# Attention in units of 32 queries of all eight heads that share keys and values

## The chip, the cores and the metric

The kernel runs on one core of a Trainium2 chip. The metric is the device time of one execution in microseconds (us), 794.44 as the median of three runs of the kernel before. A core has five engines with a queue each, which run side by side and wait for each other by semaphores: TensorE (PE; its weight loads are shown as PEld), VectorE (DVE), ScalarE (ACT), GpSimd (POOL) and SyncE (SP, which issues DMAs).

## What is computed

One layer: a norm, attention over a sliding window of 128 keys, a gated output projection, an embedding stage with a gate, and a last norm. 512 positions of width 2048, 32 query heads of 64, four heads of keys and values, so that eight query heads share each (`SWA_GROUP`). What the change touches is the attention and the projection of its queries:

```
q, k, v, gate = jnp.split(h @ w_in, [...], axis=-1)
q = q.reshape(bsz, nb, BLOCK, SWA_KV_HEADS, SWA_GROUP, SWA_HEAD_DIM)
...
scores = jnp.einsum('bnqhgd,bnjhd->bnhgqj', q, kb).astype(jnp.float32) * (SWA_HEAD_DIM ** -0.5) + bias
scores = jnp.where(mask, scores, jnp.finfo(jnp.float32).min)
m = jnp.maximum(scores.max(axis=-1, keepdims=True), sink)
e = jnp.exp(scores - m)
probs = e / (e.sum(axis=-1, keepdims=True) + jnp.exp(sink - m))
out = jnp.einsum('bnhgqj,bnjhd->bnqhgd', probs.astype(vb.dtype), vb).reshape(bsz, seq, SWA_WIDTH)
return (out * jax.nn.silu(gate)) @ w_out
```

A query sees itself and the 127 keys before it.

## The kernel before

Nearly every product is taken three times, with operands split in a high and a low part (`mm3`, lines 123 to 128: high by high, high by low, low by high). ScalarE makes the high part (a cast), VectorE the low part (a subtraction).

*Start.* A loop over 16 slices of the input projects the first two pairs of query heads, all keys (`kt`) and all values, up to 71 us. A pair of heads is one "c" of 16. `evac_q` (line 315) takes a projected pair from PSUM in three parts: `scaled` on VectorE, then the high parts on ScalarE and the low ones on VectorE, into the tile `Q[d]` of two pairs (four heads).

*Projections and attention together.* `projections()` walks over the other 14 query pairs and 16 gates; `kinds` gives their order. One step is one slice of the 2048 rows, three matmuls of 512 columns; a projection has 16 steps. Its weights come in pieces of 8 steps: a DMA of 512 KB into one of three buffers (`wraw`), a cast (`whi`, L109) and a subtraction (`wlo`, L110). What must be done once a projection ends are `chores` of three parts: of a query pair those of `evac_q`, of a gate a product on VectorE (L626), a tanh on ScalarE (L627) and a product on VectorE (L620).

Attention is cut into 64 units of 64 queries of four heads: eight groups `d` of four heads, with eight units `g` each. A loop of 67 rounds (`for i in range(blocks + 3)`) writes the order of the engines out by hand. After 16 steps ahead, a round holds

- `turn(i - 2)`: two transposes of a unit's probabilities (`pt`), ScalarE's high and VectorE's low part (`r`), a masked copy of it for queries whose window crosses a block's end (`own`, GpSimd's `affine_select`, then a copy of half of it on ScalarE, L567);
- `weigh(i - 3)`: values' products, stationary V, moving `r`, 256 columns: high, low, and one with `own` where there is one (48 units of 64); after every second unit the two halves are added into `U` (L594, L596);
- `scores(i)`: two products, stationary 32 queries of four heads, moving up to 160 keys with high and low parts side by side (320 columns), then bias, minimum, exponential, reciprocal and, a round later, the product with the reciprocal (`pr`, L532);
- seven projection steps, and between them a weight piece, chores, the later parts of the above, and DMAs that copy and sum weights in DRAM for the output stages (`sum_weights`).

PE, SP, DVE, ACT and POOL all follow the written order here. `gate_value` (L610) multiplies a gate with `U` as soon as both are there. Then come two stages of matmuls with the output and gate weights (`unit`, `Pieces`), where a scheduler orders ScalarE and VectorE.

*Buffers.* `whole` has four quarters of 8 KB a partition: after the first norm they hold `misc` (bias vector, first queries), `values`, `diffs` (differences of neighbouring value blocks, for `own`) and later the four gates. Tile `t` (scores) has three buffers, `pr` three, `r` and `own` two, `U` three.

Of the kernel before, what the change touches and what calls it, by code (L numbers as in the profile page):

```python
# [11 lines left out]
F32 = mybir.dt.float32  # L12
F32R = mybir.dt.float32r
AF = mybir.ActivationFunctionType
ALU = mybir.AluOpType
# [12 lines left out]

TWOS = PAIRS // 2
HB = P // 2  # L30
UNITS = S // HB
QB = P // 4
# [23 lines left out]
def trunk_kernel(ctx: ExitStack, tc: tile.TileContext, a: dict):  # L56
# [74 lines left out]
    sinkb = const.tile([P, TWOS], F32, name="sinkb")  # L131
# [49 lines left out]
    q_at = {int(0.5 + 3.516 * (c // 2)) - 3 + c % 2: c for c in range(2, PAIRS)}  # L181
    kinds, g = [], 0
    for m in range(2 * PAIRS - 2):
        if m in q_at:
            kinds.append(("q", q_at[m]))
        else:
            kinds.append(("g", g))
            g += 1
# [10 lines left out]
    for k in range(KC):  # L199
# [106 lines left out]
        if k == 10:  # L306
            for h in range(4):
                nc.sync.dma_start(sinkb[QB * h : QB * h + QB], a["sinks"][h].partition_broadcast(QB))
            nc.sync.dma_start(pn, a["ple_norm"])
# [5 lines left out]
    def evac_q(c, ps, to=None):  # L315


        to = ps if to is None else to
        d, u = divmod(c, 2)
        if u == 0:  # L320
            Q[d] = kvq.tile([P, S // QB, 4, QB], F32R, tag="q", name=f"q{d}", bufs=2)
        halves = slice(0, 64), slice(64, 128)

        def scaled():
            nc.vector.scalar_tensor_tensor(out=to, in0=ps, scalar=HD ** -0.5, in1=rb, op0=ALU.mult, op1=ALU.mult)

        def split(low):
            for e in range(2):
                src = to[halves[e]].rearrange("p (s q) -> p s q", q=QB)
                hi, lo = Q[d][halves[e], :, 2 * u + e], Q[d][halves[1 - e], :, 2 * u + e]  # L330
                if low:
                    nc.vector.tensor_sub(lo, src, hi.bitcast(F32))
                else:
                    nc.scalar.copy(hi, src)

        return scaled, partial_of(split, False), partial_of(split, True)
# [10 lines left out]
    misc = quarter("misc")  # L347
    first_q = [evac_q(c, q_ps[c], misc[:, 3 * c]) for c in range(2)]
# [35 lines left out]
    full = quarter("values").rearrange("p k (t c) -> p (k t) c", t=2)  # L384
# [10 lines left out]
    relb, tvec = misc[:HEADS, 1, :BUCKETS], misc[:HEADS, 2, :TOEP]  # L395
# [23 lines left out]
    U, T, PT, O, gates, biases = {}, {}, {}, {}, {}, {}  # L419
# [3 lines left out]
    diffs = {}  # L423

    def make_diff(n):
        if n == 1:
            diffs["all"] = quarter("diffs").rearrange("p k t -> p (k t)")
# [25 lines left out]
    def load_bias(d):  # L453
        biases[d] = apool.tile([P, KEYS], F32, tag="bias", name=f"bias{d}", bufs=2)
        for h in range(4):
            src = bass.AP(
                tensor=tdram.tensor, offset=tdram.offset + (4 * d + h) * TOEP + P - QB, ap=[[1, QB], [1, KEYS]]
            )
            nc.sync.dma_start(biases[d][QB * h : QB * h + QB], src)

    def scores(i):
# [6 lines left out]
        if g == 4 and d + 1 < TWOS:  # L468
            load_bias(d + 1)
        of_keys = K[d // 2].rearrange("p j l k -> p (j l k)")  # L470

        s_ps = spsum.tile([P, 2, S], F32, tag="w", name=f"s{i}")
        number = [min(2 * g + u + 1, 5) * QB for u in range(2)]
        for u in range(2):
            first, n = max(2 * g + u - 4, 0), number[u]
            st = Q[d][:, 2 * g + u].rearrange("p h q -> p (h q)")
            nc.tensor.matmul(s_ps[:, u, : 2 * n], st, of_keys[:, first * 2 * QB : (first * QB + n) * 2], start=True, stop=True)  # L477
        W = KEYS + 2
        t = apool.tile([P, 2, W], F32, tag="t", name=f"t{i}", bufs=3)
# [9 lines left out]
        late = QB if g >= 2 else 0  # L489
# [9 lines left out]
        if g < 2:  # L499
# [14 lines left out]
        if g >= 2:  # L514
# [11 lines left out]
        T[i] = apool.tile([P, 2, P], F32, tag="pr", name=f"pr{i}", bufs=3)  # L526
        for u in range(2):
            out, src = T[i][:, u], pr[u]
            if late and (g + u) % 2:
                out = out.rearrange("p (h k) -> p h k", h=2)[:, ::-1]  # L530
                src = src.rearrange("p (h k) -> p h k", h=2)
            nc.scalar.mul(out, src, sm[:, 4 + u : 5 + u])  # L532

    def turn(i):
# [8 lines left out]
        r = apool.tile([P, 2, 256], F32R, tag="r", name=f"r{i}", bufs=2)  # L543
        rh, rl = (r[:, l].rearrange("p (h u q) -> p u h q", h=4, u=2) for l in range(2))
        src = pt.rearrange("p (u h q) -> p u h q", u=2, h=4)
# [3 lines left out]
        own = None  # L549
        if g >= 2:  # L550
            own = apool.tile([P, 2, 256], F32R, tag="own", name=f"own{i}", bufs=2)
            rows = slice(0, P) if g % 2 else slice(0, HB)
            flat = lambda v: v[rows].rearrange("p l (u q) -> p (l u) q", q=HB)


            sign = -1 if g % 2 else 1
            nc.gpsimd.affine_select(  # L557
                out=flat(own), in_=flat(r).bitcast(F32), pattern=[[0, 8], [sign, HB]], compare_op=ALU.is_ge, fill=0.0,
                base=-HB - 1 if g % 2 else 0, channel_multiplier=-sign,
            )  # L560
        PT[i] = (r, own)
        yield
        if own is not None:
            here, there = slice(HB, P), slice(0, HB)
            if g % 2 == 0:
                here, there = there, here
            nc.scalar.copy(own[there, 0], own[here, 1].bitcast(F32))  # L567

    def weigh(i):

        d, g = divmod(i, UNITS)
        n, b = divmod(g, 2)
        kv = d // 2
        r, own = PT.pop(i)
        if g == 0:
            U[d] = apool.tile([P, 2, S], F32, tag="u", name=f"u{d}", bufs=3)
        if b == 0:
            O[d] = bank(f"o{i}", "o").rearrange("p (b u e q) -> p b u e q", b=2, u=2, e=2)
        ops = O[d]
        out = ops[:, b].rearrange("p u e q -> p (u e q)")  # L580
# [8 lines left out]
        if b:  # L589
            dst = U[d][:, :, n * P : (n + 1) * P].rearrange("p u (b q) -> p b u q", b=2)  # L590
            lower, upper = slice(0, 64), slice(64, 128)
            tmp = [apool.tile([P, 2, 2, HB], F32, tag=f"tmp{e}", name=f"tmp{e}_{i}", bufs=1) for e in range(2)]
            for e, (o, x) in enumerate(((lower, upper), (upper, lower))):
                nc.scalar.copy(tmp[e][o], ops[x, :, :, e, :])  # L594
            for e, o in enumerate((lower, upper)):
                nc.vector.tensor_add(dst[o], ops[o, :, :, e, :], tmp[e][o])  # L596
        if g == UNITS - 1:
            for c in (2 * d, 2 * d + 1):
# [8 lines left out]
    def gate_value(c):  # L607
# [3 lines left out]
            out=src, in0=src, scalar=0.5, in1=U[c // 2][:, c % 2], op0=ALU.mult, op1=ALU.mult  # L611
# [260 lines left out]

    nc.scalar.mul(sinkb, sinkb, -1.0)  # L873
# [3 lines left out]
    for n in range(KC):  # L877
# [3 lines left out]
    blocks = TWOS * UNITS  # L881
# [11 lines left out]
    left = KC * (len(kinds) - 1)  # L893

    def some(of, n=1):
        for _ in range(min(n, len(of))):
            of.pop(0)()

    softmax = iter(())
    for i in range(blocks + 3):  # L900
# [3 lines left out]
        value = weigh(i - 3) if 3 <= i else iter(())  # L904
        next(turned, None)
        next(value, None)
# [504 lines left out]
def laid_out(i):  # L1411
# [28 lines left out]
        "sinks": f(np.asarray(i["swa_sinks"])[0].reshape(TWOS, 4).T),  # L1440
# [19 lines left out]
```

## Time and profile before

| | |
|---|---|
| median of 3 runs (793.89 to 794.51) | 794.44 us |
| the profiled execution | 794.82 us |
| its span, first to last instruction | 793.1 us |
| granted TensorE clock | 0.997 |
| DMA moved | 185.23 MB, 234 GB/s on average |

A page of the profile gives each engine's busy time, the chain of work that ended last, and groups of equal instructions with count, busy time and mean. A row of a timeline reads: start in us from the span's start, duration, engine, line, operation, out<-in, shape, count. Rows of matmuls overlap in time, since one starts before the one ahead has drained. "[x <-y]" is idle time of the engine before the row and what ended it. The rows themselves stand in the prediction.

### The profile page before, as it was taken

The numbers are of one execution on the slowest core, as the hardware profiler recorded it, in microseconds if no ns is written. First come the engines' busy times: TensorE is split into PE (matmuls) and PEld (weight loads), VectorE is DVE, ScalarE is ACT, GpSimd is POOL, SyncE is SP. The second block draws the span as 40 slices with busy tenths as digits, with TensorE's granted clock in tenths as the row PEclk, the third lists the DMA queues.
The fourth block names the chain that finished last, engine by engine and source line by source line (L and its number), as shares of the span: only waits on it lengthen the run. The fifth ranks groups of instructions, "written<-read, shape, count | busy, mean of one in ns | idle before, by whom it ended". The sixth has DMA issues, their size and how long they took to land.

```text
span 793.1 us, 11181 instructions
## 1 busy us (share of the span) xinstructions
PE 783.2 (99%) x3746; PEld 656.0 (83%) x3746; DVE 585.7 (74%) x1155; ACT 506.7 (64%) x1067; POOL 148.5 (19%) x248
## 2 busy tenths in 40 slices
PE   9999999999999999999999999999999999999995
PEld 8888888888888888888888888888888888888885
DVE  4547587867867587767777899778866757988896
ACT  6743576666767586766666654466699656656765
POOL 0200423242413324132324200000000120210000
PEclk9999999999999999999999999999999999999998
DMA  9977999897989989898987498667864996787533
GB/s 349 275 215 264 207 275 303 223 267 215 277 227 269 223 249 258 230 247 235 244 227 182 140 365 337 197 212 232 275 237 142 346 203 202 157 225 220 176 107 106
DMA packets 45066, 185.23 MB, mean 234 GB/s; under 512 B 6656, under 2 KB 7680, under 8 KB 39888
## 3 DMA queue, kind: packets, MB, share of 16 engines
q1 hardware_dynamic: 36928, 143.30, 53.0%
q0 software_dynamic: 8080, 41.22, 27.1%
q8 instruction: 29, 0.48, 0.2%
q14 instruction: 29, 0.24, 0.1%
HBM read 177.63 MB, written 62.97 MB: 303 GB/s over the span
## 4 chain that ended last, share of the span: by engine, by line
PE 99%; DVE 0%; ACT 0%; ACTq 0%; issue 0%; DVEq 0%
PE gps L126 7%; PE gps L127 7%; PE gps L128 7%; PE qps L126 7%; PE qps L127 7%; PE qps L128 7%; PE o L127 6%; PE g L128 6%; PE g L127 5%; PE o L126 5%; PE o L128 5%; PE g L126 5%; PE s L477 2%; PE o L583 2%; PE vps L290 2%; PE pt L541 2%
## 5 line engine op out<-in xcount | busy, mean ns | idle before, releaser
L728 DVE TENSOR_TENSOR blo<-braw,bhi 128x1024 fp32r<-128x1024 f32 x102 | 124.4, 1222 | 40.9 <-ACT bhi L727 40.6
L727 ACT CAST bhi<-braw 128x1024 fp32r<-128x1024 f32 x102 | 107.3, 1052 | 72.2 <-PE o L128 24.8
L126 PE MATMUL gps<-xh,whi 128*128 128x512 f32 x256 | 100.0, 390 | 0.0
L127 PE MATMUL gps<-xl,whi 128*128 128x512 f32 x256 | 99.9, 390 | 0.0
L128 PE MATMUL gps<-xh,wlo 128*128 128x512 f32 x256 | 99.8, 390 | 0.0
L126 PE MATMUL qps<-xh,whi 128*128 128x512 f32 x224 | 87.8, 392 | 0.0
L127 PE MATMUL qps<-xl,whi 128*128 128x512 f32 x224 | 87.4, 390 | 0.0
L128 PE MATMUL qps<-xh,wlo 128*128 128x512 f32 x224 | 87.3, 390 | 0.0
L110 DVE TENSOR_TENSOR wlo<-wraw,whi 128x1024 fp32r<-128x1024 f32 x60 | 73.7, 1229 | 6.1 <-ACT whi L109 5.9
L547 DVE TENSOR_TENSOR r<-pt,r 128x256 fp32r<-128x256 f32 x64 | 27.2, 424 | 66.5 <-ACT r L546 65.6
L546 ACT CAST r<-pt 128x256 fp32r<-128x256 f32 x64 | 23.9, 373 | 80.9 <-PE pt L541 80.8
L126 PE MATMUL g<-bhi,fhg 128*128 128x512 f32 x192 | 75.1, 391 | 0.0
L126 PE MATMUL o<-bhi,fho 128*128 128x512 f32 x192 | 74.8, 390 | 0.0
L128 PE MATMUL g<-bhi,flg 128*128 128x512 f32 x192 | 74.8, 389 | 0.0
L127 PE MATMUL o<-blo,fho 128*128 128x512 f32 x192 | 74.8, 389 | 0.0
L128 PE MATMUL o<-bhi,flo 128*128 128x512 f32 x192 | 74.7, 389 | 0.0
L127 PE MATMUL g<-blo,fhg 128*128 128x512 f32 x192 | 74.7, 389 | 0.0
L557 POOL TENSOR_SCALAR_AFFINE_SELECT own<-r 64x512 fp32r<-64x512 f32 (+1 forms) x48 | 32.5, 677 | 224.6 <-DVE r L547 208.7
L109 ACT CAST whi<-wraw 128x1024 fp32r<-128x1024 f32 x60 | 62.2, 1039 | 5.4 <-issue 4.0
L492 POOL COPY t<-sinkb 128x2 f32<-128x2 f32 x64 | 53.2, 839 | 57.7 <-ACT sinkb L873 32.4
L707 POOL DMA_DIRECT2D grown<-in_ple_gate x16 | 13.8, 861 | 231.0 <-DVE blo L728 226.7
L128 PEld LDWEIGHTS gps<-xh,wlo 128*128 128x128 f32 x256 | 48.1, 188 | 10.3
(228 smaller groups left out, 1800.3 us busy)
## 6 DMA issues: line engine op xcount, KB each, us to landing
wraw<-in_w_gate_in SPq DMA_DIRECT2D x32, 512.0 KB, 6.5
w_out<-in_w_out POOLq DMA_DIRECT2D x32, 512.0 KB, 8.0
braw<-w_out SPq DMA_DIRECT2D x32, 512.0 KB, 4.4
wraw<-in_w_q SPq DMA_DIRECT2D x28, 512.0 KB, 5.3
braw<-in_ple_gate SPq DMA_DIRECT2D x24, 512.0 KB, 4.1
braw<-in_w_out SPq DMA_DIRECT2D x22, 512.0 KB, 4.2
xw<-in_first SPq DMA_DIRECT2D x14, 640.5 KB, 6.4
w_out<-in_w_out SPq DMA_DIRECT2D x16, 512.0 KB, 10.1
```

Source lines behind the costliest of these rows:

```text
L109: nc.scalar.copy(hi, raw)
L110: nc.vector.tensor_sub(lo, raw, hi.bitcast(F32))
L126: nc.tensor.matmul(ps, sh, mh, start=first, stop=False, skip_group_check=more)
L127: nc.tensor.matmul(ps, sh, ml, start=False, stop=False, skip_group_check=more)
L128: nc.tensor.matmul(ps, sl, mh, start=False, stop=last, skip_group_check=more)
L290: nc.tensor.matmul(v_ps[t], h[:, c], part_of(high_at, 256, 512), start=f, stop=e, skip_group_check=True)
L492: nc.gpsimd.tensor_copy(two(0, W + W - 1 if late else W, 1), sinkb[:, d : d + 1].unsqueeze(1).to_broadcast([P, 2, 1]))
L546: nc.scalar.copy(rh, src)
L547: nc.vector.tensor_sub(rl, src, rh.bitcast(F32))
L557: nc.gpsimd.affine_select(out=flat(own), in_=flat(r).bitcast(F32), pattern=[[0, 8], [sign, HB]], compare_op=ALU.is_ge, fill=0.0, base=-HB ...
L727: nc.scalar.copy(hi, raw)
L728: nc.vector.tensor_sub(lo, raw, hi.bitcast(F32))
```

## The change

Units become 32 queries of all eight heads that share keys and values: four groups `kv` with 16 units each, again 64 units. A score product has 16 queries of eight heads as stationary operand, and sees up to 144 keys (288 columns). Two units together make 64 queries of eight heads, and their values' products take 512 columns at once, every second round. `evac_q` now gathers four pairs of heads; for groups 0 and 2 the queries lie in two quarters of `whole`, which doubles the number of instructions for the parts. The order of the projections changes: all queries of the first group come first, 40 steps instead of 16 stand ahead of the loop, and a round holds six steps up to round 21 and seven from then on. In a round the values' products stand ahead of the transposes.

```diff
+GROUP = HEADS // KVH
+QB = P // GROUP
+TQ = 2 * QB
+UNITS = S // TQ
...
+    order = "qqqqqgqggqgqqqggqgqqqg" + "g" * 8
...
-        d, u = divmod(c, 2)
+        kv, u = divmod(c, 4)
         if u == 0:
-            Q[d] = kvq.tile([P, S // QB, 4, QB], F32R, tag="q", name=f"q{d}", bufs=2)
+            if kv % 2:
+                tiles = [kvq.tile([P, 4 * S * 2], F32R, tag="q", name=f"q{kv}")]
+            else:
+                tiles = [quarter(f"q{kv}_{n}").rearrange("p k t -> p (k t)").bitcast(F32R) for n in range(2)]
+            Q[kv] = [v.rearrange("p (s h q) -> p s h q", h=GROUP, q=QB) for v in tiles]
...
             for e in range(2):
+                for part, of in enumerate(Q[kv]):
...
-        number = [min(2 * g + u + 1, 5) * QB for u in range(2)]
+        number = [min(2 * g + u + 1, GROUP + 1) * QB for u in range(2)]
...
-        t = apool.tile([P, 2, W], F32, tag="t", name=f"t{i}", bufs=3)
+        t = apool.tile([P, 2, W], F32, tag="t", name=f"t{i}", bufs=2)
...
-            out, src = T[i][:, u], pr[u]
-            if late and (g + u) % 2:
+            out, src, w = T[i][:, u], pr[u], sm[:, 4 + u : 5 + u]
+            ahead = 2 * (g + u) % GROUP * QB if late else 0
+            if ahead == P // 2:
                 out = out.rearrange("p (h k) -> p h k", h=2)[:, ::-1]
...
+            else:
+                nc.scalar.mul(out[:, ahead:], src[:, : P - ahead], w)
+                if ahead:
+                    nc.scalar.mul(out[:, :ahead], src[:, P - ahead :], w)
...
-        r = apool.tile([P, 2, 256], F32R, tag="r", name=f"r{i}", bufs=2)
+        j, part = divmod(i, 2)
+        if part == 0:
+            own = None
+            if g >= P // TQ:
+                own = apool.tile([P, 2, S], F32R, tag="own", name=f"own{j}")
+            PT[j] = apool.tile([P, 2, S], F32R, tag="r", name=f"r{j}"), own
...
-    def weigh(i):
+    def weigh(j):
...
+        out = bank(f"o{j}", "o")
         first = V[0 if n == 0 else n - 1 + b][:, kv]
         for low in range(2):
             nc.tensor.matmul(out, first, r[:, low], start=low == 0, stop=own is None and low == 1)
...
-    for n in range(KC):
+    AHEAD = 5 * KC // 2
+    for n in range(AHEAD):
         next(proj)
         if n % 4 == 3 and W.todo:
             W.todo.pop(0)()
-    blocks = TWOS * UNITS
+        if n > KC and n % 2:
+            some(chores)
+    blocks = KVH * UNITS
...
-        value = weigh(i - 3) if 3 <= i else iter(())
+        value = weigh(i // 2 - 2) if 4 <= i and i % 2 == 0 else iter(())
+        next(value, None)
         next(turned, None)
-        next(value, None)
         next(softmax, None)
```

What this makes of the queues, at three places. First TensorE, before, at the start of a round in the second group of heads (`gps` and `qps` are projections, `s` scores):

```order
L128 MATMUL gps_1608<-xh_492,wlo_1597 128x512
L541 MATMUL pt_1697<-ident,pr_1648 128x128 x2
L583 MATMUL o_1703<-r_1631,V_716 128x256 x2
L585 MATMUL o_1703<-own_1646,DV 128x256
L477 MATMUL s_1707<-k_721,q_1022 128x320 x2
L126 MATMUL gps_1608<-xh_528,whi_1596 128x512
```

and in the changed kernel the starts of rounds 24 and 25, the first with the values of two units, the second with none:

```order
L586 MATMUL o_2376<-r_2262,V_730 128x512 x2
L588 MATMUL o_2376<-own_2261,DV 128x512
L546 MATMUL pt_2380<-ident,pr_2332 128x128 x2
L478 MATMUL s_2396<-k_1362,q_1086 128x288 x2
L126 MATMUL qps_2307<-xh_492,whi_2285 128x512
```

```order
L128 MATMUL qps_2446<-xh_142,wlo_2347 128x512
L546 MATMUL pt_2451<-ident,pr_2402 128x128 x2
L478 MATMUL s_2456<-k_1362,q_1086 128x288 x2
L126 MATMUL qps_2446<-xh_184,whi_2346 128x512
L127 MATMUL qps_2446<-xl_185,whi_2346 128x512
```

Values' products moved from every round to every second, ahead of the transposes, with twice the columns.

Second ScalarE, before, in a round with a weight cast, the high parts of a query pair and the copy of `own`:

```order
L546 CAST r_2196<-pt_2193 128x2x4x32
L532 ACTIVATE pr_2210<-t_2139,sm_2146 128x128
L532 ACTIVATE pr_2210<-t_2139,sm_2146 128x2x64
L109 CAST whi_2223<-wraw_2155 128x1024
L334 CAST q_2034<-qps_2035 64x16x32 x2
L567 CAST own_2208<-own_2208 64x256
```

and in the changed kernel in round 25:

```order
L557 CAST r_2384<-pt_2451 128x2x8x16
L535 ACTIVATE pr_2462<-t_2399,sm_2406 128x128
L535 ACTIVATE pr_2462<-t_2399,sm_2406 128x96
L537 ACTIVATE pr_2462<-t_2399,sm_2406 128x32
L109 CAST whi_2476<-wraw_2414 128x1024
L336 CAST q_0_2136<-qps_2307 64x16x16
L336 CAST q_1_2137<-qps_2307 64x16x16
L336 CAST q_0_2136<-qps_2307 64x16x16
L336 CAST q_1_2137<-qps_2307 64x16x16
L574 CAST own_2383<-own_2383 64x8x32
```

The high parts, still ahead of the copy of `own`, are four casts instead of two.

Third VectorE in the same two rounds. Before, from the end of the round ahead (its reciprocal is L523):

```order
L596 TENSOR_TENSOR u_2071<-o_2072,tmp_17_2169 64x2x2x64
L325 SCALAR_TENSOR_TENSOR qps_2035<-qps_2035,rb 128x512
L523 RECIPROCAL sm_2146<-sm_2146 128x2
L547 TENSOR_TENSOR r_2196<-pt_2193,r_2196 128x2x4x32
L507 TENSOR_TENSOR t_2206<-s_2203,bias_1636 128x2x160
```

and in the changed kernel within round 25:

```order
L516 TENSOR_TENSOR t_2459<-t_2459 128x2x16
L110 TENSOR_TENSOR wlo_2477<-wraw_2414,whi_2476 128x1024
L325 SCALAR_TENSOR_TENSOR qps_2307<-qps_2307,rb 128x512
L334 TENSOR_TENSOR q_0_2136<-qps_2307,q_0_2136 64x16x16
L334 TENSOR_TENSOR q_1_2137<-qps_2307,q_1_2137 64x16x16
```

The scaling of the query pair (L325), on which the high parts wait, stood a round ahead of them and now stands behind the weight split of the same round. In round 41 it is the same with two casts of 64x32x16.

More of the change, by code (lines that the diff above doesn't have):

```diff
@@ L177, in rsqrt_mean @@
         nc.vector.tensor_mul(out, y, t)
[L181 to L188, printed above, removed]
+    order = "qqqqqgqggqgqqqggqgqqqg" + "g" * 8
+    number = {"q": iter(range(2, PAIRS)), "g": iter(range(PAIRS))}
+    kinds = [(kind, next(number[kind])) for kind in order]
+    assert len(kinds) == 2 * PAIRS - 2
     for kind, c in kinds:
@@ L306, in trunk_kernel @@
         if k == 10:
-            for h in range(4):
+            for h in range(GROUP):
                 nc.sync.dma_start(sinkb[QB * h : QB * h + QB], a["sinks"][h].partition_broadcast(QB))
@@ L498, in scores @@
         sm = apool.tile([P, 24], F32, tag="sm", name=f"sm{i}", bufs=4)
-        if g < 2:
+        if not late:
             for u, n in enumerate(number):
@@ L513, in scores @@
             )
-        if g >= 2:
+        if late:
             nc.vector.tensor_tensor(
@@ L564, in turn @@
             here, there = slice(HB, P), slice(0, HB)
-            if g % 2 == 0:
+            if not b:
                 here, there = there, here
-            nc.scalar.copy(own[there, 0], own[here, 1].bitcast(F32))
-    def weigh(i):
[L571 to L580, printed above, removed]
+            nc.scalar.copy(flat(own, there)[:, :GROUP], flat(own, here)[:, GROUP:].bitcast(F32))
+    def weigh(j):
+        kv, m = divmod(j, S // HB)
+        n, b = divmod(m, 2)
+        r, own = PT.pop(j)
+        if m == 0:
+            U[kv] = apool.tile([P, 4, S], F32, tag="u", name=f"u{kv}", bufs=2)
+        out = bank(f"o{j}", "o")
         first = V[0 if n == 0 else n - 1 + b][:, kv]
@@ L588, in weigh @@
         yield
[L589 to L598, printed above, removed]
+        ops = out.rearrange("p (u e q) -> p u e q", u=4, e=2)
+        dst = U[kv][:, :, m * HB : (m + 1) * HB]
+        lower, upper = slice(0, 64), slice(64, 128)
+        tmp = [apool.tile([P, 4, HB], F32, tag=f"tmp{e}", name=f"tmp{e}_{j}") for e in range(2)]
+        for e, (o, x) in enumerate(((lower, upper), (upper, lower))):
+            nc.scalar.copy(tmp[e][o], ops[x, :, e, :])
+        for e, o in enumerate((lower, upper)):
+            nc.vector.tensor_add(dst[o], ops[o, :, e, :], tmp[e][o])
+        if m == S // HB - 1:
+            for c in range(4 * kv, 4 * kv + 4):
                 weighed.add(c)
@@ L871, in projections, with some @@
                 yield
+    def some(of, n=1):
+        for _ in range(min(n, len(of))):
+            of.pop(0)()
     nc.scalar.mul(sinkb, sinkb, -1.0)
@@ L891, in sums_in @@
         return range(SUMS_EARLY + (i - 4) * n // of, SUMS_EARLY + (i - 3) * n // of)
[L893 to L897, printed above, removed]
+    left = KC * len(kinds) - AHEAD
     softmax = iter(())
```

77 lines of the change are left out of this document (36 added, 41 removed).

## The prediction

> **What bounds it now.** First the page and the list of TensorE's waits.
>
> ```profile
> span 793.1 us, 11181 instructions
> PE 783.2 (99%) x3746; PEld 656.0 (83%) x3746; DVE 585.7 (74%) x1155; ACT 506.7 (64%) x1067; POOL 148.5 (19%) x248
> PE 99%; DVE 0%; ACT 0%; ACTq 0%; issue 0%; DVEq 0%
> PE warm_ps L141 <- PEq L1450: 0.8, 1, 0.8
> ```
>
> TensorE is busy for 99% of the span, the chain that ended last is TensorE throughout, and its only listed wait is 0.8 us at the start. So a matmul saved is time saved, unless another engine then makes TensorE wait. Next I read one whole round, from the transposes of one unit to those of the next, in the timeline.
>
> ```profile
> 299.60 0.38 PE L541 MATMUL pt<-ident,pr 128*128 128x128 f32 x2
> 299.73 0.48 PE L583 MATMUL o<-r,V 128*128 128x256 f32 x2
> 300.05 0.28 PE L585 MATMUL o<-own,DV 128*128 128x256 f32 x1
> 300.17 0.46 PE L477 MATMUL s<-k,q 128*128 128x320 f32 x2
> 300.47 0.39 PE L126 MATMUL qps<-xh,whi 128*128 128x512 f32 x1
> ...
> 305.02 0.40 PE L128 MATMUL qps<-xh,wlo 128*128 128x512 f32 x1
> 305.26 0.38 PE L541 MATMUL pt<-ident,pr 128*128 128x128 f32 x2
> ...
> 305.71 0.28 PE L585 MATMUL o<-own,DV 128*128 128x256 f32 x1
> 305.83 0.34 PE L477 MATMUL s<-k,q 128*128 128x64 f32 x2
> ...
> 306.29 0.39 PE L127 MATMUL qps<-xl,whi 128*128 128x512 f32 x1
> ...
> 776.65 0.28 PE L126 MATMUL last<-last,fhg 128*128 128x256 f32 x1
> ...
> 780.60 0.28 PE L126 MATMUL last<-last,fhg 128*128 128x256 f32 x1
> ```
>
> Durations overlap here, so I price a matmul by the distance between starts. The 21 projection matmuls from 300.47 to 305.02 stand 4.55/20 = 0.2275 us apart; the 34 matmuls of 256 columns from 776.65 to 780.60 stand 3.95/33 = 0.1197 us apart. A straight line through both is 0.0119 us plus 0.000421 us a column: 0.1466 for 320 columns (the row shows (300.47 - 300.17)/2 = 0.15) and 0.1332 for 288. Very short products don't follow it: 64 and 128 columns take 306.29 - 305.83 - 0.2275 = 0.23 us together, about 0.115 each.
>
> **The change, part by part.**
>
> *Score products.* 96 products of 320 columns become 96 of 288: 96 x (0.1466 - 0.1332) = 1.29 us saved. The first products of each group of heads are 32 before and 32 after; before, 16 are of up to 128 columns (0.23 a pair) and 16 of 192 or 256; after, they go from 32 to 256. At 0.115 to 0.12 apiece both sums are 3.7 us: nothing.
>
> *Values' products.* 128 + 48 = 176 of 256 columns become 64 + 24 = 88 of 512: 176 x 0.1197 - 88 x 0.2275 = 1.05 us saved. [...]
>
> *Transposes* stay 128. A short matmul followed by a weight load costs extra: behind the transposes this round spends 299.73 to 300.05 on two products that are worth 0.24, 0.08 us too much. After the change the score product stands there. The trace has such rounds:
>
> ```profile
> 92.40 0.38 PE L541 MATMUL pt<-ident,pr 128*128 128x128 f32 x2
> 92.53 0.54 PE L477 MATMUL s<-k,q 128*128 128x320 f32 x2
> ...
> 97.70 0.38 PE L541 MATMUL pt<-ident,pr 128*128 128x128 f32 x2
> ```
>
> There the round takes 5.30 us, 21 x 0.2275 + 4 products on the line (2 x 0.066 + 2 x 0.1466) = 5.20 and 0.10 too much: the same extra, nothing saved. **TensorE's own work falls by 1.29 + 1.05 = 2.34 us**, call it 2.3.
>
> *New rounds.* Rounds without value products (odd ones) now alternate with rounds that carry 512-column ones. Those up to 21 hold six projection steps, later ones seven. By the row above, an odd round of seven steps takes 5.30 - 2 x 0.0134 = 5.27 us, one of six 4.59. The second unit of a pair gets its masked copy ("own") in the odd round, and the third matmul of the next round reads it: at 5.27 + 2 x 0.2275 = 5.73 us after the odd round's transposes (5.05 with six steps). Before, it was due at 305.71 - 299.60 = 6.11. So ScalarE has 0.38 us less. What it does in such a round:
>
> ```profile
> 300.01 0.38 ACT L546 CAST r<-pt 128x256 fp32r<-128x256 f32 x1 [1.76 <-PE pt L541]
> 300.28 0.69 ACT L532 ACTIVATE pr<-t,sm 128x128 f32<-128x128 f32 x2
> 300.88 1.04 ACT L109 CAST whi<-wraw 128x1024 fp32r<-128x1024 f32 x1
> 304.01 0.60 ACT L627 ACTIVATE gps<-gate 128x512 f32<-128x512 f32 x1 [2.09 <-DVE gate L626]
> 304.64 0.40 ACT L567 CAST own<-own 64x256 fp32r<-64x256 f32 x1
> ...
> 302.16 1.22 DVE L110 TENSOR_TENSOR wlo<-wraw,whi 128x1024 fp32r<-128x1024 f32 x1
> 303.29 0.68 DVE L626 TENSOR_TENSOR gate<-gps,rb 128x512 f32<-128x512 f32 x1
> ...
> 133.44 0.69 DVE L325 SCALAR_TENSOR_TENSOR qps<-qps,rb 128x512 f32<-128x512 f32 x1
> 134.17 1.18 ACT L334 CAST q<-qps 64x512 fp32r<-64x512 f32 x2 [1.45 <-DVE qps L325]
> ...
> L594 ACT COPY tmp<-o 64x256 f32<-64x256 f32 x64 | 23.5, 367 | 1.1
> ...
> 77.25 0.20 ACT L873 ACTIVATE sinkb<-sinkb 128x8 f32<-128x8 f32 x1
> ```
>
> The copy L567 stands behind the tanh L627, that waits for VectorE's L626, and that for the weight split L110: it ends at 305.04, 5.44 us after the transposes, 0.67 ahead of its reader. In the order of the changed kernel two odd rounds of seven steps have, behind the weight split, the scaling of a query projection on VectorE and its high parts on ScalarE, and only then the copy:
> - round 41, two casts of 64x512: 5.44 + (1.18 - 0.60) = 6.02, due at 5.73: **0.3 us of waiting**;
> - round 25 (the one shown in the order), four casts of 64x256 because this group's queries lie in two tiles. The nearest row is L594, 0.367 each: 5.44 + (1.47 - 0.60) = 6.31: **0.6 us**.
> In round 57 a tanh stands there as above: 5.44 against 5.73, no wait. In round 7 (six steps) the scaling is a round earlier, but the round before is full (weights, two key casts, two copies): I put the end at 4.9 to 5.1 against 5.05: 0 to 0.1. These waits, about **1.0 us**, are paid in full, since TensorE has nothing else queued. Bounds: zero, if the casts are shorter than L594's, and 1.8, if each costs what half of L334 does (0.59).
>
> *Edits at no cost.* A late unit's probabilities take three ScalarE instructions instead of two in 48 units. The 8-column row L873 took 0.20, so this adds 0.2 to 0.3 us a unit ahead of the weights' cast; VectorE, busy until 302.16 in that round, hides it, and without this cover it would add to the two waits. The first round starts 40 steps into the projections instead of 16:
>
> ```profile
> 71.47 0.39 PE L126 MATMUL gps<-xh,whi 128*128 128x512 f32 x1
> ...
> 82.36 0.33 PE L477 MATMUL s<-k,q 128*128 128x64 f32 x2
> ...
> 457.02 1.28 DVE L610 SCALAR_TENSOR_TENSOR gate<-gate,u 128x512 f32<-128x512 f32 x2
> 458.22 1.22 DVE L728 TENSOR_TENSOR blo<-braw,bhi 128x1024 fp32r<-128x1024 f32 x1
> ...
> 460.73 0.39 PE L127 MATMUL o<-blo,fho 128*128 128x512 f32 x1
> ```
>
> 16 steps took 10.89 us, so the last of the four queries that the first scores need is projected 32 steps in, and 8 steps (5.4 us) are left for its scaling (0.69), a weight pair (1.04 + 1.22) and its high parts (4 x 0.37, with the low ones close behind on VectorE): about 4.4, no wait. At the end four gate products fall behind the last unit instead of two, 1.28 us more on VectorE ahead of a weight split that had 460.73 - 459.44 = 1.29 us to spare; in the changed order one weight split and one form of 0.6 to 1.2 us move away from there, so about zero, at worst 0.5. Pools with fewer buffers (t, pr, r, own) are refilled one or two rounds after their last reader; the value products were moved ahead of the transposes, so the single r is free when ScalarE refills it.
>
> **Sum.** The profiled execution took 794.82 us (span 793.1). 794.82 - 2.3 + 1.0 = 793.5; it lay 0.4 above the median 794.44, so I forecast **793.2**.
>
> **Rivals.**
> - *No new wait*: the casts are quick enough, or an order of 0.1 us in each queue helps. Only the 2.3 count: 792.1. For it: no wait behind the copy is listed now. Against: 0.3 and 0.6 are missing by rows of this trace.
> - *More waits than two*: rounds of six steps are short for ScalarE, and each backlog of some 0.3 us in rounds 7, 15 and the end's 0.5 adds up to another 1.0: 794.2.
> - *Width doesn't pay*: 512 columns cost two of 256, so the change doesn't do what it says. Then only the scores gain: 1.3 saved, 1.0 waited: 794.1. Against it are the starts 0.1197 and 0.2275 apart. [...]
> - *Slower: the DMAs can't keep up with shorter rounds.* Copies and sums of weights are issued by round, and rounds 4 to 21 shrink from 305.26 - 299.60 = 5.66 us to 4.59 without and 4.59 + 3 x 0.2275 = 5.27 with value products, 4.93 on average, 13% less.
>
> ```profile
> 160.00:180.00 20.00, 20.00 (x101) 16.82 (x100) 13.27 (x42) 13.92 (x41) 9.93 (x17) 1.00 0.96 270
> ...
> 200.00:220.00 20.00, 20.00 (x100) 16.78 (x99) 16.02 (x44) 15.59 (x41) 8.35 (x14) 1.00 0.97 295
> ...
> L109 ACT CAST whi<-wraw 128x1024 fp32r<-128x1024 f32 x54 | 56.1, 1038 | 0.0
> ...
> DMA to landing us min/median/max: 4.5/9.2/14.4
> ```
>
> The DMA share is 0.96 in the first row. If the 0.97 of the second is all that can be carried, 0.96 x 5.66/4.93 = 1.10 stretches 18 rounds (89 us) by 13%, 12 us; with half of it, as the projections' weights are not issued by round, 794.44 - 2.3 + 1.0 + 6 = 799. It decides once a weight lands later than its cast is due. A weight lasts 8 steps, 8/7 of 5.66 = 6.5 us; three buffers less a split of 2.3 leave 17 us, and the longest landing is 14.4. Against: the cast L109 never waited (0.0 over 54).
>
> **Numbers.** A measurement of this kernel can tell about 0.2% (1.6 us) from no change; the line lies at 792.85. Forecast 0.45 (793.2, of it 0.07 below the line), no wait 0.27, more waits 0.12, width 0.06, slower 0.10. Faster 0.07 + 0.27 = 0.34, slower 0.10, same 0.56. The range runs from 791.8 (no wait, 0.3 of scatter) to 795.4 (waits at their bound of 1.8, the end's 0.5 and 1.0 of further ones).
>
> **What would show it.** Starts of 512-column value products 0.227 apart, scores 0.133; "o <- ACT own" in TensorE's waits, some 0.6 us near 228 us and 0.3 near 317 us, nothing elsewhere in the loop; L109 still without idle time. The prediction is wrong if those waits are absent or other ones stand in the list, or if the joined products start more than 0.235 apart.

## The result, and the profile after

| | kernel before | changed kernel |
|---|---|---|
| median | 794.48 us (793.89 to 794.77, 4 runs) | 801.74 us (800.52 to 802.57, 4 runs) |
| ratio to before, 95% interval | 1 | 1.0091 [1.0074, 1.0109] |
| the profiled execution, its span | 794.82, 793.1 us | 801.74, 800.0 us |
| granted clock | 0.997 | 0.992 |

The change made the kernel 0.9% slower; 793.2 was forecast, with a range that ended at 795.4. First the page of the changed kernel: span, the granted clock and the DMA share in 40 slices of 20 us, and the chain that ended last.

```profile
span 800.0 us, 11168 instructions
...
PEclk9999998999999999999999999999999999999998
DMA  9782699999998997989797698767873996796633
...
PE 89%; DVE 3%; DMA 3%; ACT 2%; issue 2%; POOL 0%; SPq 0%; ACTq 0%; DVEq 0%; POOLq 0%
```

The chain was TensorE for 99%; now it is 89%, with DMA, VectorE and ScalarE in it. The chain is followed back from the end: it leaves TensorE at some wait, and from there back runs over ScalarE, VectorE and a DMA. The DMA row has a hole (2 and 6 in slices 4 and 5, 60 to 100 us) just ahead of a run of nines, and the clock dips in slice 7. The list of TensorE's waits has, after "us in total, times, longest us":

```profile
PE o L586 <- ACT r L557: 5.0, 1, 5.0
...
PE o L127 <- DVE blo L731: 0.6, 1, 0.6
PE o L588 <- ACT own L574: 0.5, 2, 0.3
PE s L478 <- DVE q L334: 0.3, 1, 0.3
```

One stop of 5.0 us, not many small ones. The two waits on `own` are the ones that were forecast; the others the prediction had at nothing, or nearly so. The timeline of the changed kernel around the stop:

```profile
117.02 1.05 ACT L109 CAST whi<-wraw 128x1024 fp32r<-128x1024 f32 x1 [2.36 <-DMA wraw<-in_w_q]
...
125.92 1.05 ACT L109 CAST whi<-wraw 128x1024 fp32r<-128x1024 f32 x1 [4.82 <-DMA wraw<-in_w_gate_in]
126.05 0.39 PE L128 MATMUL qps<-xh,wlo 128*128 128x512 f32 x1
...
127.00 1.23 DVE L110 TENSOR_TENSOR wlo<-wraw,whi 128x1024 fp32r<-128x1024 f32 x1 [5.31 <-ACT whi L109]
...
128.87 1.17 ACT L336 CAST q<-qps 64x512 fp32r<-64x512 f32 x2 [1.13 <-DVE qps L325]
...
130.07 0.40 ACT L522 ACTIVATE t<-t,sm 128x129 f32<-128x129 f32 x1
...
130.97 0.37 ACT L557 CAST r<-pt 128x256 fp32r<-128x256 f32 x1
...
131.39 1.57 PE L586 MATMUL o<-r,V 128*128 128x512 f32 x2 [4.96 <-ACT r L557]
```

Read from the bottom: TensorE waits for the cast `r`. In ScalarE's queue that cast stands behind an exponential, behind a query's high parts (which wait for VectorE, busy with a weight's low part) and behind the cast of weight piece 10. For this piece ScalarE sat idle 4.82 us, because the DMA landed only at 125.9; for piece 9, at 117.0, it had sat idle 2.36 us. TensorE itself did not need that weight yet: it had done 40 + 6 x 6 = 76 steps, and piece 10 serves steps 80 to 87. Where the late DMA comes from is seen on SP's queue, before (first fence) and after (second); the rows with `small` and `w_out` are the eight copies of 512 KB each from DRAM to DRAM that round 0 issues.

```profile
66.13 1.29 SPq L689 DMA_DIRECT2D small<-in_w_out  x2
67.46 4.62 SPq L689 DMA_DIRECT2D w_out<-in_w_out  x6
```

```profile
66.69 23.40 SPq L102 DMA_DIRECT2D wraw<-in_w_q  x5
90.14 1.23 SPq L692 DMA_DIRECT2D small<-in_w_out  x2
91.41 3.96 SPq L692 DMA_DIRECT2D w_out<-in_w_out  x6
97.42 0.34 SPq L102 DMA_DIRECT2D wraw<-in_w_q  x1
106.06 2.42 SPq L440 DMA_DIRECT2D DV<-diffs  x4
108.53 0.58 SPq L102 DMA_DIRECT2D wraw<-in_w_gate_in  x1
```

With 40 steps ahead of round 0 instead of 16, the copies are issued 24 us later, behind three more weight pieces, and run beside pieces 9 (issued 97.42) and 10 (108.53), GpSimd's sums and the twelve spreads of differences (`DV`). Piece 10 also stands behind the first four spreads in SP's queue, which wait for their differences until 106.06. The stretches, with the granted clock, the DMA share and GB/s at the end of a row, before and after:

```profile
60.00:75.00 15.00, 15.00 (x73) 12.62 (x72) 9.46 (x14) 5.41 (x9) 0.00 (x0) 1.00 0.73 253
75.00:90.00 15.00, 15.00 (x70) 12.44 (x69) 11.32 (x30) 7.07 (x17) 10.85 (x18) 1.00 0.93 231
...
120.00:130.00 10.00, 10.00 (x53) 8.42 (x52) 7.86 (x23) 7.14 (x20) 5.06 (x9) 1.00 1.03 308
```

```profile
60.00:75.00 15.00, 15.00 (x73) 12.59 (x73) 11.68 (x20) 7.69 (x17) 0.00 (x0) 1.00 0.39 126
75.00:90.00 15.00, 15.00 (x68) 12.43 (x67) 11.04 (x19) 4.74 (x9) 4.52 (x10) 1.00 0.22 70
...
120.00:130.00 10.00, 6.44 (x31) 5.01 (x29) 4.59 (x14) 3.89 (x8) 0.96 (x2) 0.93 1.04 294
130.00:140.00 10.00, 8.61 (x32) 6.54 (x33) 8.04 (x24) 8.87 (x29) 2.73 (x4) 0.73 0.97 324
```

From 60 to 90 us the DMAs worked 0.83 of the time before, and 0.30 after: (0.83 - 0.30) x 30 = 16 us of their time went unused, and the work was still to be done in a stretch that is full (a share of 1.04 and 0.97 from 120 to 140 us). The weight transfers show it (the view of line L102, changed kernel; the longest landing before was 14.4):

```profile
  ACT whi L109: 8.6, 3
...
DMA to landing us min/median/max: 3.6/6.6/19.6
```

**Where the 6.9 us of span came from.** Cut the span at the first projection matmul and at the first one of the output stage. Before, these stand at 71.47 and 452.32, after at 71.08 and 458.80:

```profile
452.32 0.40 PE L126 MATMUL o<-bhi,fho 128*128 128x512 f32 x1
```

```profile
71.08 0.39 PE L126 MATMUL qps<-xh,whi 128*128 128x512 f32 x1
...
458.80 0.39 PE L126 MATMUL o<-bhi,fho 128*128 128x512 f32 x1
```

The stretch between them took 380.85 us before and 387.72 after, 6.87 more: all of it is in the loop. By the distances between TensorE's starts the parts are: the stop 5.1; slow matmuls and a second wait of 0.5 (for r's low part) behind it 2.3; the first scores 0.48; rounds 25 and 41, 0.46 + 0.12 and 0.33 + 0.12 (the copy of `own`, and the transposes behind it); 0.11 at the last unit. Together 9.0, so TensorE's own work fell by about 9.0 - 6.9 = 2.1.

### The profile page after: what moved, and what is told of

Same layout as the page of the kernel before. It is cut to its first block, busy times and chain, and to the rows that moved or that the text cites. A ratio compares the mean times of both kernels' runs of the same rounds, so it can differ in the third digit from the quotient of the medians.

```text
span 800.0 us, 11168 instructions
## 1 busy us (share of the span) xinstructions
PE 784.2 (98%) x3658; PEld 650.4 (81%) x3658; DVE 583.8 (73%) x1171; ACT 517.9 (65%) x1131; POOL 150.6 (19%) x252
## 4 chain that ended last, share of the span: by engine, by line
PE 89%; DVE 3%; DMA 3%; ACT 2%; issue 2%; POOL 0%; SPq 0%; ACTq 0%; DVEq 0%; POOLq 0%
PE gps L126 7%; PE gps L127 7%; PE gps L128 7%; PE qps L126 6%; PE qps L127 6%; PE qps L128 6%; PE g L126 5%; PE g L127 5%; PE g L128 5%; PE o L127 4%; PE o L128 4%; PE o L126 4%; DMA wraw<-in_w_gate_in 2%; PE s L478 2%; PE vps L286 2%; PE o L586 2%
## 5 line engine op out<-in xcount | busy, mean ns | idle before, releaser
L109 ACT CAST whi<-wraw 128x1024 fp32r<-128x1024 f32 x60 | 62.3, 1039 | 17.7 <-issue 9.1
L493 POOL COPY t<-sinkb 128x2 f32<-128x2 f32 x64 | 49.3, 770 | 98.9 <-ACT pr L535 34.3
L565 POOL TENSOR_SCALAR_AFFINE_SELECT own<-r 64x512 fp32r<-64x512 f32 (+1 forms) x48 | 35.4, 737 | 160.0 <-DVE r L558 151.3
```

The lines of the kernel that those rows point to most:

```text
L109: nc.scalar.copy(hi, raw)
L493: nc.gpsimd.tensor_copy(two(0, W + W - 1 if late else W, 1), sinkb[:, d : d + 1].unsqueeze(1).to_broadcast([P, 2, 1]))
L565: nc.gpsimd.affine_select(out=flat(own, rows), in_=flat(r, rows).bitcast(F32), pattern=[[0, 2 * GROUP], [sign, TQ]], compare_op=ALU.is_ge, ...
```

## The experiments

Theory A: the eight moved copies, the spreads of differences, the sums and the weight pieces are more than the DMAs carry in that stretch; a piece lands late, its cast blocks ScalarE's queue, and `r` behind it stops TensorE. Its rivals are named in the expectations. All medians:

| kernel | median, us | ratio to before, 95% interval |
|---|---|---|
| e1, copies issued ahead | 794.85 | 1.0004 [0.9994, 1.0013] |
| e2, copies and sums spread | 793.70 | 0.9993 [0.9984, 1.0003] |
| e3, no spreads of differences | 798.51 | 1.0054 [1.0039, 1.0069] |
| e4, two casts a round later | 801.50 | 1.0092 [1.0077, 1.0107] |
| e5, e2 with values' products halved | 795.16 | 1.0003 [0.9994, 1.0012] |
| e6, e2 with two reorderings | 792.12 | 0.9968 [0.9957, 0.9980] |
| e7, first sums later | 793.92 | 0.9988 [0.9979, 0.9997] |
| e8, kernel before with the copies late | 809.55 | 1.0183 [1.0166, 1.0201] |
| e9, kernel before with e2's placement | 794.36 | 1.0000 [0.9990, 1.0009] |

### e1: the copies back to where the DMAs are idle

```diff
     load_bias(0)
+    for n in range(0, SUMS_EARLY, 2):
+        sum_weights(n)
     W.apart = True
...
         if i == 0:
-            return range(0, SUMS_EARLY, 2)
+            return range(0)
```

> The changed kernel with its first eight DRAM copies of weights (8 x 512 KB) issued before the 40 steps ahead instead of behind round 0, so at about 67 to 72 us instead of 90 to 95. Theory A (the burst): these copies delay weight pieces 9 and 10 (19.6 and 17.4 us to landing), ScalarE's queue stands behind the late casts, and the cast r behind them stops TensorE for 5.1 us at 126 us, after which the granted clock costs about 2.2 more: both go, 801.7 - 7.3 = 794.4, ratio 1.000 to the kernel before, and no wait on r in TensorE's list. Theory B (shortage): the shorter rounds 4 to 21 ask for more than the DMAs carry; the late landings only move to a later round, 798 or more. Theory C (fewer buffers: one r, two t): copies have nothing to do with it, 801 to 802.

794.85: 6.9 us came back, theory A's 7.3 nearly. The wait on `r` is gone; `own` has 1.1 us of waits, one of them new. It is the copy of round 7 (its reader stood at 137.66 us), which the prediction put at 0 to 0.1; e3 has it as well and e2 has not, and why was not followed:

```profile
PE o L588 <- ACT own L574: 1.1, 3, 0.6
```

The copies delay weights in their old place too: a cast at 85.02 waited 6.67 us for its piece. But that was before round 0, with no `r` in the queue behind it, and TensorE's list has no wait there. Theory C (fewer buffers) falls: nothing was changed in the buffers, and the stop went.

### e2: the copies spread over the loop

```diff
     def sums_in(i):
-        if i == 0:
-            return range(0, SUMS_EARLY, 2)
-        if i < 4:
-            return range(4 * i + 3, min(4 * i + 7, SUMS_EARLY), 2)
-        n, of = SUM_STEPS - SUMS_EARLY, blocks - 4
-        return range(SUMS_EARLY + (i - 4) * n // of, SUMS_EARLY + (i - 3) * n // of)
+        return range(max(i - 6, 0) * SUM_STEPS // (blocks - 6), max(i - 5, 0) * SUM_STEPS // (blocks - 6))
```

> The changed kernel with no copies or sums of weights before round 6; all 94 of these steps are spread evenly over rounds 6 to 63. Theory A (the burst): pieces 9 and 10 land within 10 us, the stop at 126 us goes, 794.4 to 795. Theory B (shortage): the loop now carries the eight copies and five sums on top of the rest, so weights land late in more rounds, 798 to 803. Theory C (fewer buffers): 801 to 802.

793.70, below the 794.4 to 795 that theory A gave. Theory B, which is the slower rival of the prediction, falls here: the loop carries more than in the changed kernel, and only small waits are left (beside the 0.8 at the very start):

```profile
PE o L588 <- ACT own L574: 0.5, 2, 0.3
PE s L478 <- DVE q L334: 0.3, 1, 0.3
```

### e3: without the spreads of differences

```diff
+    nc.gpsimd.memset(DV.bitcast(F32), 0.0)
     W.apart = True
...
-        if step == 2 and 1 <= i - 1 < NB:
-            spread_diff(i - 1)
```

> The changed kernel without the twelve DMAs that spread the value differences (12 x 128 KB in rounds 2 to 4); DV is filled with zeros instead, so the products with own add nothing. The eight copies stay where they are. Theory A (the burst of 8 x 512 KB, each read and written): the spreads are 1.5 of some 10 MB moved in that stretch; pieces 9 and 10 land 2 to 4 us earlier, and the stop of 5.1 us shrinks to 1 to 3: 797 to 799.5. Theory D (the spreads are what delays piece 10): the stop goes, 794.4. Theory C (fewer buffers): 801 to 802.

798.51, within theory A's range. The stop shrank to 1.0 us, without slow matmuls behind it; smaller waits on `r`, `sm` and `own` stand beside it in the list (0.3, 0.4 and 0.6 at the most). From the list:

```profile
PE o L584 <- ACT r L555: 0.9, 1, 0.9
```

The spreads have a share in the stop, but are not its cause alone (theory D). How they take part is not what theory A says, though. Piece 10 landed at 121.7 instead of 125.9, but it was longer on its way, 20.9 us against 17.4; it came sooner because SP issued it at 100.85 instead of 108.53, with no spreads ahead of it:

```profile
100.85 10.82 SPq L102 DMA_DIRECT2D wraw<-in_w_gate_in  x2
```

So what this run shows of the spreads (1.5 MB) is their place in SP's queue; that their traffic slows the pieces is not shown. A version with the piece issued ahead of them was not tried.

### e4: the late weights' casts behind r

```diff
                 first_chores(i, 1)
-                some(W.todo)
+                if i != 3:
+                    some(W.todo)
+                if i in (3, 4):
+                    W.load(i + 8)
```

> The changed kernel with the casts and low parts of weight pieces 9 and 10 written one round later in ScalarE's and VectorE's queues (behind the cast r of that round instead of ahead of it); the DMAs are issued in the same order and all else stays. Theory A (a late weight stops TensorE only through the instructions queued behind its cast): the landings stay at 15 to 20 us, but the stop at 126 us shrinks to 1 us or less, 794 to 796. Theory E (the weight itself is what TensorE lacks): it waits for wlo or whi instead, 800 or more.

801.50: **a miss for theory A in the time, though not for the reason of its rival**. The stop at 126 us did go; TensorE ran on to 135.7 us. But two stops came back later, 0.7 us for `r` and this one, by its list and ScalarE's timeline:

```profile
PE o L588 <- ACT own L574: 4.9, 3, 4.5
```

```profile
132.15 1.05 ACT L109 CAST whi<-wraw 128x1024 fp32r<-128x1024 f32 x1 [2.90 <-DMA wraw<-in_w_gate_in]
...
139.90 1.04 ACT L109 CAST whi<-wraw 128x1024 fp32r<-128x1024 f32 x1 [1.94 <-DMA wraw<-in_w_q]
...
141.92 0.40 ACT L574 CAST own<-own 64x256 fp32r<-64x256 f32 x1
```

Now pieces 11 and 12 are late, and `own` stands behind their casts. TensorE did not wait for a weight here either, so the queue behind the cast is the way in which lateness reaches TensorE. The 5 us themselves are a debt. Piece 11 landed at 131.1 us in the changed kernel and at 132.1 here; there the stop had put its cast off to 135.40, here ScalarE stood ready for it at 129.25. Reordering ScalarE only chose where the lateness was paid.

### e7: the first sums later, the copies where they are

`sums_in` issues nothing between round 0 and round 9; the rest follows as before.

```diff
-        if i < 4:
-            return range(4 * i + 3, min(4 * i + 7, SUMS_EARLY), 2)
-        n, of = SUM_STEPS - SUMS_EARLY, blocks - 4
+        if i < 12:
+            return range(4 * (i - 8) + 3, min(4 * (i - 8) + 7, SUMS_EARLY), 2) if i > 8 else range(0)
+        n, of = SUM_STEPS - SUMS_EARLY, blocks - 12
...
```

> The changed kernel with its eight copies where they are (behind round 0) but no sums, and no further copies, before round 9: the first five sums move from rounds 1 to 3 to rounds 9 to 11, the rest is spread over rounds 12 to 63. Theory A (the sum of copies, spreads of differences, sums and weight pieces is more than the DMAs carry in that stretch, and taking any of them away frees a part): piece 9 lands 3 to 6 us earlier, piece 10 within 12 us, the stop of 5.1 us shrinks to 0 to 2: 794.5 to 797.5. Theory I (the copies alone delay the pieces): 800 to 802.

793.92, below the lower end that A gave: the stop is gone whole. The copies without the sums (theory I) make no stop: piece 9 took 11.6 us to land instead of 19.6, and piece 10 3.8 instead of 17.4, with the copies and the spreads where they were. With the copies ahead instead (e1) the two took 3.7 and 11.4. So copies and sums together slow the pieces, and the spreads put piece 10 further back. Moving or taking away any one of the three (e1, e3, e7) removes most or all of the stop. One small lateness is left further on: a cast waited 1.79 us for its piece at 198.65, and TensorE, by its distances, lost about 0.9 us at 204.6 to 206.3.

### e8 and e9: the same placements in the kernel before

In e8 the eight copies go behind round 2 and the first sums to rounds 3 to 5; in e9 `sums_in` is that of e2.

```diff
-        if i == 0:
-            return range(0, SUMS_EARLY, 2)
-        if i < 4:
-            return range(4 * i + 3, min(4 * i + 7, SUMS_EARLY), 2)
-        n, of = SUM_STEPS - SUMS_EARLY, blocks - 4
+        if i < 6:
+            i -= 2
+            return range(0, SUMS_EARLY, 2) if i == 0 else range(4 * i + 3, min(4 * i + 7, SUMS_EARLY), 2) if i > 0 else range(0)
+        n, of = SUM_STEPS - SUMS_EARLY, blocks - 6
...
```

> The kernel before, units of 64 queries and all, with its first eight copies moved from behind round 0 to behind round 2, so that they are issued at about 100 to 110 us, among the spreads of differences, instead of 66 to 72, and the first five sums moved two rounds as well. Theory A (the place of the burst makes the stop, in whatever kernel): weight pieces land later than their casts are due, ScalarE waits for a weight and TensorE for what stands behind it, 797 to 802. Theory B (it takes the shorter rounds of the changed kernel): rounds of 5.66 us leave room, 794.0 to 795.0.

809.55, more than A expected, in a kernel that has none of the new units, and longer rounds. SP issued the copies earlier than I had put it, and at nearly the same time as in the changed kernel (90.14):

```profile
90.83 1.22 SPq L689 DMA_DIRECT2D small<-in_w_out  x2
```

The mechanism is the same down to the rows (ScalarE's timeline, then TensorE's list):

```profile
116.74 1.04 ACT L109 CAST whi<-wraw 128x1024 fp32r<-128x1024 f32 x1 [12.37 <-DMA wraw<-in_w_gate_in]
...
118.46 0.40 ACT L567 CAST own<-own 64x256 fp32r<-64x256 f32 x1
```

```profile
PE o L585 <- ACT own L567: 12.7, 3, 10.3
```

So the place of the burst, with the sums behind it, makes a stop without the new units.

> The kernel before with the placement of e2: no copies or sums of weights before round 6, all spread evenly over rounds 6 to 63. It tells how much of the 0.997 of e6 comes from the placement and how much from units of 32 queries. Theory K (the kernel before never waited for a DMA, so the placement alone brings nothing): 794.0 to 794.9, ratio 0.9995 to 1.0005; the units then bring all of e6's 2.5 us. Rival (emptying the start brings something by itself, or the fuller loop costs something): outside 793.6 to 795.4.

794.36, theory K: the placement by itself is worth nothing where no DMA was late.

### e6: the two forecast waits and the one at the start taken away

```diff
             elif n == 2:
+                if i % 2:
+                    next(turned, None)
                 next(value, None)
...
-        if n % 4 == 3 and W.todo:
+        if (n % 4 == 3 or n == 2 * KC) and W.todo:
             W.todo.pop(0)()
```

> The version with the copies spread (e2, 793.7, span 791.6), with two reorderings. In odd rounds ScalarE's copy of own is written ahead of a query's high parts; at the start the split of weight piece 6 is written before the high parts of the last query instead of between its high and low parts. Theory: the waits on own at about 227 and 317 us (0.46 and 0.33, with 0.11 and 0.12 behind them) and the one on q at 97.6 us (0.48) go, 1.5 us: span 790.1, 792.2, ratio 0.997 to the kernel before. Rival: the copy of own stands ahead of ready work while GpSimd's select is not done, and a query's high and low parts come later; what goes here comes back as another wait, 793.5 or more.

792.12, where 792.2 was expected; the only wait left in TensorE's list is the 0.8 at the very start. This is the fastest version, 0.32% [0.20, 0.43] ahead of the kernel before. By e9 the placement has no part in that. What the units, with their waits removed, give in the loop is read from the rows:

```profile
70.88 0.39 PE L126 MATMUL qps<-xh,whi 128*128 128x512 f32 x1
...
449.73 0.39 PE L126 MATMUL o<-bhi,fho 128*128 128x512 f32 x1
```

Its loop takes 449.73 - 70.88 = 378.85 us against 380.85: with no wait on either side, TensorE's work fell by 2.0. The other 0.6 between the two profiled starts lies ahead of the loop, where executions with the same code differ as much: e2 and e5 start it at 70.61 and 71.17.

### e5: what the joined products are worth

```diff
+        for c in (slice(0, 256), slice(256, 512)):
+            for low in range(2):
+                nc.tensor.matmul(out[:, c], first, r[:, low, c], start=low == 0, stop=own is None and low == 1)
...
```

> The version with the copies spread (e2, 793.7, span 791.6), with each values' product of 512 columns taken as two of 256, as many products as in the kernel before. Theory F, the price that the prediction took from the projections (512 columns 0.2275 apart, 256 columns 0.1197): 176 x 0.1197 - 88 x 0.2275 = 1.05 us more, span 792.7. Theory G, the trace of the changed kernel, where the joined products stand 0.233 to 0.236 apart: 176 x 0.1197 - 88 x 0.235 = 0.4 more, span 792.0. If the two halves cost no more than the whole: 791.6.

Span 793.5, 1.9 more than e2, beyond every theory. The time is no clean measure: 0.6 of it lies ahead of the first projection matmul (71.17 against 70.61 us), and the waits on `own` grew from 0.5 to 1.0, since its reader now comes sooner. The distances are one. In e2 two joined products take 294.49 - 294.02 = 0.47; in e5 four halves take 295.81 - 295.32 = 0.49:

```profile
294.02 0.63 PE L586 MATMUL o<-r,V 128*128 128x512 f32 x2
294.49 0.38 PE L546 MATMUL pt<-ident,pr 128*128 128x128 f32 x2
```

```profile
295.32 0.66 PE L587 MATMUL o<-r,V 128*128 128x256 f32 x4
295.81 0.38 PE L546 MATMUL pt<-ident,pr 128*128 128x128 f32 x2
```

Over all, by the medians of the start distances, 88 joined products take 20.75 us (0.236 each) and 176 halves 21.55 (0.1225 each): 0.8 us, between theories F and G. Against the kernel before, where a half stands 0.119 from the next, the joining gained less still (next section).

## The prediction, point by point

**What failed** is the step "Edits at no cost", in the sentence "The first round starts 40 steps into the projections instead of 16". It followed what the first scores wait for, and not what else round 0 issues: eight copies of 512 KB, on SP's queue behind three more weight pieces, out of a stretch in which the DMAs had room (a share of 0.39 and 0.22 without the copies) into one in which they had little (0.86 to 1.03 between 90 and 130 us already in the kernel before). Costed at nothing, it cost 7.4 us: 5.1 of stop and 2.3 behind it. Without it (e2) the changed kernel takes 793.70, 0.5 from the forecast; there is luck in that nearness, since the saved work came out 0.3 lower and the waits 0.5 higher than forecast, 0.8 together.

**The slower rival had the right condition and the wrong place.** "It decides once a weight lands later than its cast is due" is what happened, 19.6 us against the 17 worked out. (The 17 is no sharp edge: landings of 17.6 in e2 and 18.1 in e6 held up no cast.) But it looked for a steady shortage over rounds 4 to 21, and took the idle-free cast L109 of the kernel before as evidence against it. That evidence held only for the copies where they were. e2 and e6 carry the whole load in the shorter rounds without such a wait, and e7 with one of 1.79 us; the burst at rounds 0 to 5 needs no shorter rounds (e8).

**The saved work** was put at 2.34 and measured at 2.0 to 2.1, with its two terms mis-sized against each other, so that their errors in part cancelled by luck. By the sums of the distances from start to start, in the kernel before and in e6, where nothing in the loop waits: scores 17.55 and 20.79 us, values 26.01 and 20.81. Together they fell by 1.96, which is the loop's 2.0. In this the extra of 0.083 behind the transposes went from the values to the scores, as the prediction said (in the kernel before, the first product behind the transposes starts at 299.73, the weight load of the second at 299.82 and the second at 299.93, 0.20 behind the first instead of 0.12): 63 of them left the values (5.2 us), and the scores have 61 more than before (5.1). Without it the scores saved 17.55 + 5.1 - 20.79 = 1.9 (1.29 forecast), of which the 96 wide products give 1.5 and the short first ones, put at nothing, most of the rest; and the values saved 26.01 - 5.2 - 20.81 = 0.0 (1.05 forecast). The wrong choice was the row of the trace: 0.2275 comes from the long accumulations of the projections, while the joined values' products stand 0.233 to 0.236 apart, at the edge (0.235) that the prediction set itself; why they are slower was not tried. The rival "width doesn't pay" was thus right on this term.

**The two waits on `own`** were forecast at 0.6 (round 25) and 0.3 (round 41), none in round 57: measured 0.46 and 0.33, each with 0.12 behind it, and none in round 57. Their sum of 1.0 is right, and e6 removed them by the order alone, so the queue behind the query's high parts is shown as the cause.

**The start's own wait** was forecast at none, and is 0.48. The step put the low parts "close behind" the high ones; the rows of the changed kernel have a weight's low part between:

```profile
93.05 0.70 DVE L325 SCALAR_TENSOR_TENSOR qps<-qps,rb 128x512 f32<-128x512 f32 x1 [3.31 <-PE qps L128]
96.17 1.23 DVE L110 TENSOR_TENSOR wlo<-wraw,whi 128x1024 fp32r<-128x1024 f32 x1 [2.43 <-ACT whi L109]
97.43 1.53 DVE L334 TENSOR_TENSOR q<-qps,q 64x256 fp32r<-64x256 f32 x4
```

From 93.05 to 98.96 are 5.9 us, where 5.4 were there and 4.4 reckoned. With the weight's split written first (e6), the wait is gone.

**The end** was "about zero, at worst 0.5": 0.6 in the profiled execution of the changed kernel (VectorE's `blo` in the list above), none listed in e1 to e7. One execution each; why it differs was not followed. **The pools with fewer buffers** cost nothing that e6's list would show.

## What to carry to other kernels

When a step is moved along a hand-written order, write down every DMA that it issues and look up the DMA share of the stretch that it leaves and of the one that it enters, and what stands ahead of each weight in the queue that issues it: the eight copies left 794.85 us where the DMA share was 0.39 and 0.22 without them (e1), and 801.74 where it was 0.92 to 1.04 with them. A late transfer need not be late for its reader to stop the kernel (piece 10, cast at 125.92 for steps 80 to 87, stopped TensorE for 5.0 us behind step 76); what counts is what stands behind the first instruction that waits for it, and putting that instruction further back only moved the stop here, with the transfers as they were (e4, 801.50 against 801.74). And price a product by a row of products with the same operands' pattern, not by the commonest row of its width (0.236 measured for 512 columns, 0.2275 taken).

## What the runs showed of the hardware

Behind the stop of 5.1 us TensorE ran at about half pace: 512 columns stand 0.43 us apart instead of 0.2275, up to about 135.5, some 4 us after it started again.

```profile
133.94 0.63 PE L126 MATMUL qps<-xh,whi 128*128 128x512 f32 x1
134.37 0.63 PE L127 MATMUL qps<-xl,whi 128*128 128x512 f32 x1
```

The granted clock of that stretch (130 to 140 us) is 0.73 in the windows above. The same followed the stop of 10.3 us in e8: from 119.83 to 123.24 us 512 columns stand 0.426 apart, and the clock is 0.66 and 0.82 in the windows of 110 to 120 and 120 to 130 us. In e4, with its stop of 4.5 us, the mean clock of the profiled execution is 0.992, as in the changed kernel. In e3, with a stop of 1.0, it is 0.997, and around e8's stop of 1.7 us, from 130 to 150 us, the clock is 1.00. What makes it, and from which length of stop on, no run shows. The stop of 5.1 us thus cost 7.4, with a second wait of 0.5 in it.

Sums that GpSimd issues slowed weight pieces that SP issues: in the changed kernel a piece of 512 KB took 3.6 us at best, and piece 10 took 17.4 beside the sums, at a DMA share of 0.98 to 1.04 (100 to 130 us); with the sums later (e7) it took 3.8, at 0.90 and 0.64 (100 to 120 us).
